# Hybrid attention block on one core: six transpose sources, two maximum tiles, four remainder buffers, remainder products one key tile behind, memory keys and values in reused buffers

## The chip, the core and the metric

The kernel runs on one core of a Trainium2 chip. Its engines are TensorE (PE; its weight loads are listed apart as PEld), VectorE (DVE), ScalarE (ACT), GpSimd (POOL) and SyncE (SP, which here only issues transfers). Each engine works through its own list of instructions in order and waits at an instruction until what it needs is there. The metric is the device time of one launch in microseconds (us).

## What is computed

One decoder layer on x of 2048 tokens by 1024 channels. After a normalisation, one input projection feeds three attention branches and a gate; the branches are concatenated, multiplied by the gate and mapped back.

```python
h = rms_norm(x, norm_g)
cq, ckv, kr, dq, dk, dv, mq, z = split(h @ w_in)
y_mla  = mla_branch(cq, ckv, kr, ...)    # 8 heads, causal, keys of 96, values of 64
y_diff = diff_branch(dq, dk, dv, ...)    # 4 heads, two causal softmax maps each, keys of 32
y_mem  = mem_branch(mq, mem, ...)        # 4 heads over 256 memory tokens
y = concat(y_mla, y_diff, y_mem) * silu(z)
x = x + y @ w_out
```

## The kernel before

**Precision by splitting.** Operands are split into a 16-bit high part and a 16-bit remainder, and a product is made of two or three matmuls.

**Steps.** Attention runs in steps, each for one block of 512 queries (b = 0 to 3): four for the memory branch (m00 to m03), eight for the differential branch (d00 to d13) and sixteen for the latent branch (a00 to a33: four pairs of heads by four blocks). A step first has a preparation (`prep_m`, `prep_d`, `prep_a`): it projects, normalises and rotates, copies queries and keys as 16-bit sources (`ks`, `qs`, and for the other branches `s`, `qa`), turns them with transposing DMAs issued by SP, and estimates row maxima (`est_block`), which are written into the query source before it is transposed a second time. Then come the step's maps, one for each head or softmax map.

**Units.** A map (`class Map`) goes over key tiles of 128. For each one, `head` makes the scores `st` on PE (three matmuls of 512 columns in the latent branch, one in the differential branch), ACT takes the exponential into `p32` (L492), and DVE subtracts its 16-bit view `phi` to leave the remainder `plo` (L493). `tail` then multiplies on PE: eight matmuls of 64 or 65 columns from `phi` (L502, L504) and four from `plo` (L507), all into one accumulator `pv`. Two heads are emitted ahead of each tail (`DEPTH = 2`).

**Rings.** Tiles of one tag share a fixed number of buffers; a tile's first writer waits until the tile that had the buffer is done with. All transpose sources share the tag `s2` with 5 buffers (`stack`). In `prep_a` a source is first touched by POOL, which fills its padding (L855, L861), and then by ACT, which copies the high part (L856 for keys, L862 for queries):

```python
ks = stack([P, 4, 2, P], f"ks{h}_{nm}")
G.memset(ks[:, :, :, 96:128], MS)
A.activation(ks[:, :, 0, 0:96], kn[:, :, h], AF.Copy)
...
qs = stack([P, 2, 4, P], f"qs{h}_{nm}")
G.memset(qs[:, :, :, 96:128], 0.0)
A.activation(qs[:, 0, :, 0:96], q[:, :, h], AF.Copy)
```

The same POOL queue computes the inverse norms `r_a` (L97, L101), for which DVE's scaling of the keys `kn_a` waits (L847). The maximum tile `er` has one buffer: ACT writes the first copy of the estimated scores into it (L390), DVE takes maxima over it (L394, L398, L399). `plo` has three buffers, `p32` three, `st` two, `pv` one. The pool `kvp` has two rings of five: `kT` (transposed keys, `qA` of the memory branch, early weight stages) and `V`.

**Order.** Work outside the maps (preparations, projections, output products) is cut into pieces with planned positions, and the pieces are interleaved with the units by position and priority. From that the framework's scheduler sets the order of each engine's list when the kernel is built, so a change of buffers or of emission order changes the order of all lists.

The memory branch's keys `mk1`, `mk2` and values `mv` lie in buffers of their own for the whole kernel.

Of the kernel before, what the change touches and what calls it, by code (L numbers as in the profile page):

```python
# [11 lines left out]
F32 = mybir.dt.float32  # L12
F16 = mybir.dt.float16
BF16 = mybir.dt.bfloat16
# [5 lines left out]
P = 128  # L20
# [20 lines left out]
def hybrid_block(ctx: ExitStack, tc: tile.TileContext, x, mem, positions, norm_g, w_in, mla_q_norm_g,  # L41
# [3 lines left out]
    V, A, G, T, SP = nc.vector, nc.scalar, nc.gpsimd, nc.tensor, nc.sync  # L45

    cst = ctx.enter_context(tc.tile_pool(name="cst", bufs=1))
# [8 lines left out]
    ps_v = ctx.enter_context(tc.tile_pool(name="ps_v", bufs=1, space=bass.MemoryType.PSUM))  # L56

    def stack(shape, name):
        return wk.tile(shape, F16, tag="s2", name=name, bufs=5)

    def bigt(shape, name):
        return big.tile(shape, F16, tag="big", name=name)
# [134 lines left out]
    g_mk = gain_row(mem_kn_g, 64, "g_mk")  # L197
    g_mq = gain_row(mem_qn_g, 64, "g_mq")
    V.tensor_tensor(g_mk, g_mk, g_mq, ALU.mult)
    mk1 = cst.tile([P, 2, 4, P], F16, name="mk1")  # L200
    mk2 = cst.tile([P, 2, 4, P], F16, name="mk2")
    mv = cst.tile([P, 2, 4, 130], F16, name="mv")

    mem_left = [0]

    def mem_kv():
        units = []
        xts = []
        for t in range(2):
            xts.append(fetch_rows(mem[0, t * P:(t + 1) * P, :], f"m{t}", big, MPACE))  # L210
            yield 1.0
        yield from load_w(w_mem_kv, [(0, 512)], gm, "mkv", units, kvp, pace=MPACE)
        hts = []
        for t in range(2):
            hts.append(normed_t(xts[t], f"m{t}"))
            yield 1.0
        kv = tmp4("mem_kv").rearrange("p (t c) -> p t c", t=2)
        for t in range(2):
            ps = ps_p.tile([P, 512], F32, tag="pp", name="pp")
            project(ps, hts[t], units, 512)  # L220
            A.activation(kv[:, t, :], ps, AF.Copy, scale=1.0 / WS)
            yield 5.0
        sq = tmp4("mem_sq")[:, 0:512].rearrange("p (t c) -> p t c", t=2)
        A.activation(sq, kv[:, 0:2, 0:256], AF.Square, scale=1.0 / 8.0)
        ss = sm.tile([P, 8], F32, tag="yss", name="mem_ss")
        V.reduce_sum(ss[:, 0:8], sq.rearrange("p t (h d) -> p (t h) d", d=64), axis=AX.X)
        r = rstd_of(ss[:, 0:8], [8], "mem_r", "rstd_x")
        kn = tmp4("mem_kn")[:, 0:512].rearrange("p (t h d) -> p t h d", t=2, d=64)
        rr = _bc(r.rearrange("p (t h) -> p t h", h=4), 3, 64)
        V.tensor_tensor(kn, kv[:, 0:2, 0:256].rearrange("p t (h d) -> p t h d", d=64), rr, ALU.mult)  # L230
        kn = kn.rearrange("p t h d -> p (t h) d")
        V.tensor_tensor(kn, kn, _bc(g_mk, 1, 8), ALU.mult)
        s1 = stack([P, 8, 2, 64], "mem_s1")
        s2 = stack([P, 8, 128], "mem_s2")
        A.activation(s1, _bc(kn, 2, 2), AF.Copy)
        V.tensor_tensor(s2[:, :, 0:64], kn, s1[:, :, 0, :], ALU.subtract)
        G.memset(s2[:, :, 64:128], MS)
        SP.dma_start_transpose(mk1.rearrange("p t h k -> p (t h) k"), s1.rearrange("p a b c -> p (a b c)"))
        SP.dma_start_transpose(mk2.rearrange("p t h k -> p (t h) k"), s2.rearrange("p a c -> p (a c)"))
        vv = kv[:, 0:2, 256:512].rearrange("p t (h d) -> p t h d", d=64)  # L240
        A.activation(mv[:, :, :, 0:64], vv, AF.Copy)
        V.tensor_tensor(mv[:, :, :, 65:129], vv, mv[:, :, :, 0:64], ALU.subtract)
        G.memset(mv[:, :, :, 64:65], WS)
        mem_left.clear()
        yield 1.0
# [127 lines left out]
    def est_block(st, i, nmap, mcol, lhs, rhs):  # L373
        b = st.b
        mx = sm.tile([P, nmap, 4, 2], F32, tag="mx", name=f"mx{i}_{st.name}", bufs=2)
        fold = b >= EB
        for m in range(nmap):
            for t in range(4):
                if fold and t % 2 == 0:
                    er = wk.tile([P, 2, 512], BF16, tag="er", name="er", bufs=1)  # L380
                for c in range(b + 1):
                    ps = ps_e.tile([P, 512], F32, tag="pe", name="pe")
                    n = (4 if c < b else t + 1) * P
                    T.matmul(ps[:, 0:n], lhsT=lhs(m, t), rhs=rhs(m, c, n // P), start=True, stop=c < b)  # L384
                    if c == b:
                        T.matmul(ps[:, t * P:n], lhsT=ident, rhs=mask_e, start=False, stop=True)
                    if not fold:
                        V.reduce_max(mx[:, m, t, c:c + 1], ps[:, 0:n], axis=AX.X)
                    elif c == 0:
                        A.activation(er[:, t % 2], ps, AF.Copy)  # L390
                    else:
                        ec = wk.tile([P, 512], BF16, tag="ec", name="ec", bufs=3)
                        A.activation(ec[:, 0:n], ps[:, 0:n], AF.Copy)  # L393
                        V.tensor_tensor(er[:, t % 2, 0:n], er[:, t % 2, 0:n], ec[:, 0:n], ALU.max)  # L394
                    yield 0.5
                if fold and t % 2:
                    for n in (256, 128, 64):
                        V.tensor_tensor(er[:, :, 0:n], er[:, :, 0:n], er[:, :, n:2 * n], ALU.max)  # L398
                    V.reduce_max(mx[:, m, t - 1:t + 1, 0], er[:, :, 0:64], axis=AX.X)  # L399
        if b == 1 and not fold:  # L400
            mr = sm.tile([P, nmap * 4], F32, tag="mr", name=f"mr{i}_{st.name}", bufs=2)
            V.reduce_max(mr, mx.rearrange("p m t c -> p (m t) c"), axis=AX.X)
            mr = mr.rearrange("p (m t) -> p m t", t=4)
        else:
            mr = mx[:, :, :, 0]
        for m in range(nmap):
            V.tensor_scalar_mul(mcol(m), mr[:, m, :], -1.0 / MS)
# [66 lines left out]
    class Map:  # L474
# [9 lines left out]
        def head(self, j):  # L484
            t0 = max(0, j - self.diag0)
            n = (4 - t0) * P
            ps = ps_s.tile([P, 512], F32, tag="st", name="st")
            self.scores(ps, j, t0, n, j >= self.diag0)
            p32 = wk.tile([P, 512], F32, tag="p32", name="p32", bufs=3)
            plo = wk.tile([P, 512], F16, tag="plo", name="plo", bufs=3)  # L490
            phi = p32.bitcast(BF16).rearrange("p (n t) -> p n t", t=2)[:, :, 1]
            A.activation(p32[:, :n], ps[:, :n], AF.Exp, scale=self.scale)  # L492
            V.tensor_tensor(plo[:, :n], p32[:, :n], phi[:, :n], ALU.subtract)  # L493
            return t0, phi, plo

        def tail(self, j, t0, phi, plo):
            if j == 0:
                self.pv = ps_v.tile([P, 4, P], F32, tag="pv", name="pv")
            pvv, vt = self.pv, self.vtile(j)
            for t in range(t0, 4):  # L500
                c = slice((t - t0) * P, (t - t0 + 1) * P)
                T.matmul(pvv[:, t, 0:65], lhsT=phi[:, c], rhs=vt[:, 0:65], start=(j == 0 and t == 0), stop=False,  # L502
                         skip_group_check=True)
                T.matmul(pvv[:, t, 0:64], lhsT=phi[:, c], rhs=vt[:, 65:129], start=False, stop=False, skip_group_check=True)  # L504
            for t in range(t0, 4):
                c = slice((t - t0) * P, (t - t0 + 1) * P)
                last["pv"] = T.matmul(pvv[:, t, 0:65], lhsT=plo[:, c], rhs=vt[:, 0:65], start=False,  # L507
                                      stop=(j == self.njt - 1), skip_group_check=True)
            if j < self.njt - 1:
                return None  # L510
            rl = sm.tile([P, 4], F32, tag="rl", name="rl", bufs=4)
            V.reciprocal(rl, pvv[:, :, 64])
            return self.done(pvv[:, :, 0:64], rl)

    def new_ys(ct, b):
        return wk.tile([P, 2, 4, P], F16, tag="ys", name=f"ys{ct}_{b}", bufs=1)
# [106 lines left out]
    def est_m(st):  # L623
# [6 lines left out]
        for i in range(2):  # L630
            for t in range(4):
                ps = ps_e.tile([P, 512], F32, tag="pe", name="pe")
                for k in range(2):
                    T.matmul(ps[:, 256 * k:256 * k + 256], lhsT=st.qA[:, i, t, k, :], rhs=mk1[:, :, 2 * i + k, :],
                             start=(k == 0), stop=(k == 1), skip_group_check=True)
                V.reduce_max(mx[:, i, t, :], ps.rearrange("p (i k) -> p i k", i=2), axis=AX.X)
                yield 0.5
# [6 lines left out]
    def maps_m(st):  # L644
# [7 lines left out]
        for h in range(4):  # L652

            def scores(ps, j, t0, n, diag, h=h):
                T.matmul(ps, lhsT=mk1[:, j, h, :], rhs=st.qA[:, h // 2, :, h % 2, :], start=True, stop=False)
                T.matmul(ps, lhsT=mk2[:, j, h, :], rhs=st.qB[h // 2][:, :, h % 2, :], start=False, stop=True)

            def done(o, rl, h=h):
                hp, i = h // 2, h % 2
# [578 lines left out]
```

## Time and profile before

| | |
|---|---|
| median of 3 runs | 1416.08 us (1415.18 to 1417.94) |
| profiled execution | 1417.06 us, its span 1415.3 us |
| PE busy | 1309.6 us, 93% of the span |
| DVE busy | 1117.0 us, 79% |
| ACT busy | 898.2 us, 63% |
| POOL busy | 358.9 us, 25% |
| granted TensorE clock, mean | 0.977 |

The span runs from the first to the last instruction of the profiled execution; 1.8 us of its time lie around it. A busy share is an average over stages. A granted clock of 1.00 is 2.4 GHz, and the other level is 1.2 GHz; a mean between them over a stretch is a share of each.

### The profile page before, as it was taken

What the parts mean: (1) busy time and instruction counts of PE and PEld (TensorE: products, weight loads), DVE (VectorE), ACT (ScalarE), POOL (GpSimd) and SP (SyncE); (2) the same over time, 40 slices, a digit from 0 to 9 for tenths busy, and PEclk for the clock granted to TensorE, in tenths of its full rate; (3) what the DMA queues carried; (4) which work ended last, traced back from release to release, by engine and by line L of the source; (5) the groups of instructions that cost most, each with busy time, mean ns of one, the idle gap of its engine ahead of it and who ended that gap; (6) DMA issues with size and microseconds to landing.
All of it is one profiled execution on the core that took longest, in us unless ns stands there. A gap on an engine that the chain in (4) does not pass through costs nothing.

```text
span 1415.3 us, 35199 instructions
## 1 busy us (share of the span) xinstructions
PE 1309.6 (93%) x13552; PEld 833.7 (59%) x13552; DVE 1117.0 (79%) x2649; ACT 898.2 (63%) x2153; POOL 358.9 (25%) x541
## 2 busy tenths in 40 slices
PE   4889899999999999998998999999998988999998
PEld 1344455667677666667775655666655655565554
DVE  3558787889888867888898888887889987985745
ACT  4646444687787646786885766766776777674521
POOL 2222133304063133104212143252333332300000
PEclk9999999999999999999999999999999998999999
DMA  8999754224213313437345156346434443255452
GB/s 203 252 213 194 163 102 98 53 61 87 55 31 69 69 32 59 76 106 194 113 89 137 47 151 173 69 98 146 117 91 94 115 81 72 54 128 168 130 190 76
DMA packets 302697, 157.67 MB, mean 111 GB/s; under 512 B 248385, under 2 KB 281281, under 8 KB 302529
## 3 DMA queue, kind: packets, MB, share of 16 engines
q1 hardware_dynamic: 302496, 155.42, 46.9%
q8 instruction: 106, 1.74, 0.5%
q14 instruction: 63, 0.51, 0.1%
q0 software_dynamic: 32, 0.00, 0.0%
HBM read 61.79 MB, written 34.34 MB: 68 GB/s over the span
## 4 chain that ended last, share of the span: by engine, by line
PE 51%; DMA 12%; DVE 12%; POOL 11%; ACT 8%; issue 5%; SPq 2%; ACTq 0%; DVEq 0%; POOLq 0%
PE pp L176 6%; PE pp L177 5%; PE pp L178 5%; PE pe L384 5%; DMA kT_a<-ks_a 3%; DVE plo L493 3%; PE pv L507 3%; PE pv L504 3%; PE pp L932 3%; PE pv L502 3%; PE pp L934 3%; PE pp L933 3%; PE st L548 2%; POOL r_a L101 2%; PE st L892 2%
## 5 line engine op out<-in xcount | busy, mean ns | idle before, releaser
L492 ACT ACTIVATE p<-st 128x512 f32<-128x512 f32 (+3 forms) x672 | 356.4, 547 | 183.1 <-PE st L894 64.5
L493 DVE TENSOR_TENSOR plo<-p 128x512 f16<-128x512 f32 (+3 forms) x672 | 406.7, 616 | 63.0 <-ACT p L492 54.0
L393 ACT ACTIVATE ec<-pe 128x512 bf16<-128x512 f32 (+3 forms) x384 | 198.3, 534 | 35.8 <-PE pe L384 14.8
L502 PEld LDWEIGHTS <-p 128*128 128x128 bf16 x2304 | 186.7, 100 | 47.3 <-issue 7.4
L504 PEld LDWEIGHTS <-p 128*128 128x128 bf16 x2304 | 177.2, 99 | 31.3 <-issue 2.1
L507 PEld LDWEIGHTS <-plo 128*128 128x128 f16 x2304 | 135.3, 99 | 56.5 <-DVE plo L493 22.4
L394 DVE TENSOR_TENSOR er<-er,ec 128x512 bf16<-128x512 bf16 (+3 forms) x384 | 143.7, 380 | 30.3 <-ACT ec L393 20.3
L390 ACT ACTIVATE er<-pe 128x512 bf16<-128x512 f32 x192 | 110.4, 606 | 39.7 <-DVE mx_d L399 13.9
L176 PEld LDWEIGHTS <-ht_x 128*128 128x128 f16 x896 | 88.1, 98 | 73.2 <-DMA ht_x<-xh_x 21.1
L892 PE MATMUL st<-qB_a,kT_a 97*128 97x512 f16 (+1 forms) x320 | 113.0, 353 | 18.4 <-ACT p L492 17.2
L502 PE MATMUL pv<-V_d,p 128*128 128x65 f16 x1088 | 119.9, 195 | 2.7 <-DVE y_d L559 2.4
L177 PEld LDWEIGHTS <-ht_x 128*128 128x128 f16 x896 | 88.2, 98 | 57.3 <-issue 11.8
L548 PE MATMUL st<-qB_d,kT_d 97*128 97x512 f16 (+1 forms) x320 | 112.5, 355 | 9.9 <-ACT p L492 8.8
L504 PE MATMUL pv<-V_d,p 128*128 128x64 f16 x1088 | 120.0, 197 | 0.0
L178 PEld LDWEIGHTS <-ht_x 128*128 128x128 f16 x896 | 88.1, 98 | 53.8 <-issue 4.1
L502 PE MATMUL pv<-V_a,p 128*128 128x65 f16 x1088 | 116.5, 194 | 1.2 <-ACT p L492 0.9
L504 PE MATMUL pv<-V_a,p 128*128 128x64 f16 x1088 | 116.2, 196 | 0.0
L893 PE MATMUL st<-qB_a,kT_a 96*128 96x512 f16 (+1 forms) x320 | 113.1, 354 | 0.0
L894 PE MATMUL st<-qB_a,kT_a 96*128 96x512 f16 (+1 forms) x320 | 112.4, 351 | 0.0
L384 PE MATMUL pe<-kT_d,qB_d 96*128 96x512 f16 (+2 forms) x320 | 106.6, 351 | 5.9 <-ACT ec L393 2.9
L384 PE MATMUL pe<-kT_a,qB_a 96*128 96x512 f16 (+2 forms) x320 | 102.0, 358 | 6.9 <-DMA qB_a<-qs_a 3.1
L507 PE MATMUL pv<-V_a,plo 128*128 128x65 f16 x1088 | 89.5, 195 | 9.6 <-DVE plo L493 9.2
(285 smaller groups left out, 3363.7 us busy)
## 6 DMA issues: line engine op xcount, KB each, us to landing
xt_x<-in_x_dram SPq DMA_DIRECT2D x16, 512.0 KB, 4.7
xr<-in_x_dram SPq DMA_DIRECT2D x16, 512.0 KB, 3.6
part<-xr SPq DMA_DIRECT2D x16, 512.0 KB, 2.9
ysc<-yt SPq DMA_DIRECT2D x31, 256.0 KB, 2.2
yl<-ysc SPq DMA_DIRECT2D x15, 512.0 KB, 4.3
zsc<-zc SPq DMA_DIRECT2D x48, 128.0 KB, 2.1
xa<-part SPq DMA_DIRECT2D x12, 512.0 KB, 3.6
out_dram<-xa SPq DMA_DIRECT2D x12, 512.0 KB, 2.9
```

The source lines that it names most:

```text
L176: T.matmul(ps[:, :n], lhsT=ht[:, 0, k], rhs=wt[:, 0, :n], start=(k == 0), stop=False)
L177: T.matmul(ps[:, :n], lhsT=ht[:, 0, k], rhs=wt[:, 1, :n], start=False, stop=False)
L178: T.matmul(ps[:, :n], lhsT=ht[:, 1, k], rhs=wt[:, 0, :n], start=False, stop=(k == NK - 1))
L384: T.matmul(ps[:, 0:n], lhsT=lhs(m, t), rhs=rhs(m, c, n // P), start=True, stop=c < b)
L393: A.activation(ec[:, 0:n], ps[:, 0:n], AF.Copy)
L394: V.tensor_tensor(er[:, t % 2, 0:n], er[:, t % 2, 0:n], ec[:, 0:n], ALU.max)
L492: A.activation(p32[:, :n], ps[:, :n], AF.Exp, scale=self.scale)
L493: V.tensor_tensor(plo[:, :n], p32[:, :n], phi[:, :n], ALU.subtract)
L502: T.matmul(pvv[:, t, 0:65], lhsT=phi[:, c], rhs=vt[:, 0:65], start=(j == 0 and t == 0), stop=False, skip_group_check=True)
L504: T.matmul(pvv[:, t, 0:64], lhsT=phi[:, c], rhs=vt[:, 65:129], start=False, stop=False, skip_group_check=True)
L507: last["pv"] = T.matmul(pvv[:, t, 0:65], lhsT=plo[:, c], rhs=vt[:, 0:65], start=False, stop=(j == self.njt - 1), skip_group_check=True)
L892: T.matmul(ps[:, :n], lhsT=kt[0:97, h, j % 4, 0, :], rhs=q[0:97, 0, t0:4, :], start=True, stop=False)
```

## The change

Five edits. The transpose sources get six buffers, `er` two and `plo` four. In `tail`, the four `plo` products of a key tile are no longer issued behind that tile's `phi` products but behind those of the next tile; the last tile of a map issues both (new method `low`). The memory keys become one tile `mk12` in the ring `kT` and the values a tile in the ring `V`. No instruction is added or removed on any engine: the numbers of matmuls, vector, scalar and GpSimd operations and transfers are the same.

```diff
     def stack(shape, name):
-        return wk.tile(shape, F16, tag="s2", name=name, bufs=5)
+        return wk.tile(shape, F16, tag="s2", name=name, bufs=6)
...
-    mk1 = cst.tile([P, 2, 4, P], F16, name="mk1")
-    mk2 = cst.tile([P, 2, 4, P], F16, name="mk2")
-    mv = cst.tile([P, 2, 4, 130], F16, name="mv")
+    mk = []
+    mv = kvp.tile([P, 2, 4, 130], F16, tag="V", name="mv", bufs=5)
...
+        mk12 = kvp.tile([P, 2, 2, 4, P], F16, tag="kT", name="mk12")
+        mk.extend([mk12[:, 0], mk12[:, 1]])
...
-                    er = wk.tile([P, 2, 512], BF16, tag="er", name="er", bufs=1)
+                    er = wk.tile([P, 2, 512], BF16, tag="er", name="er", bufs=2)
...
-            plo = wk.tile([P, 512], F16, tag="plo", name="plo", bufs=3)
+            plo = wk.tile([P, 512], F16, tag="plo", name="plo", bufs=4)
...
+            if self.late is not None:
+                self.low(*self.late)
+            self.late = (j, t0, plo)
+            if j < self.njt - 1:
+                return None
+            self.low(*self.late)
+            rl = sm.tile([P, 4], F32, tag="rl", name="rl", bufs=4)
+            V.reciprocal(rl, pvv[:, :, 64])
+            return self.done(pvv[:, :, 0:64], rl)
+
+        late = None
+
+        def low(self, j, t0, plo):
+
+            pvv, vt = self.pv, self.vtile(j)
             for t in range(t0, 4):
                 c = slice((t - t0) * P, (t - t0 + 1) * P)
                 last["pv"] = T.matmul(pvv[:, t, 0:65], lhsT=plo[:, c], rhs=vt[:, 0:65], start=False,
                                       stop=(j == self.njt - 1), skip_group_check=True)
```

**First place, PE in step a13.** The matmuls of PE's list around two key tiles of one map; tiles are named by their numbers, and the exponential and the remainder of one key tile have neighbouring numbers (`p32_18319` and `plo_18320`). Weight loads and the further `phi` and `plo` products of a tile are left out. Before:

```order
L502 MATMUL pv_18283<-V_a10_14947,p32_18319 128x65
L504 MATMUL pv_18283<-V_a10_14947,p32_18319 128x64
...
L507 MATMUL pv_18283<-V_a10_14947,plo_18320 128x65
...
L892 MATMUL st_18389<-qB1_a13_17066,kT_a11_15928 128x512
L893 MATMUL st_18389<-qB1_a13_17066,kT_a11_15928 128x512
L894 MATMUL st_18389<-qB1_a13_17066,kT_a11_15928 128x512
```

Now, the same key tile (its remainder is `plo_18315` here, its exponential was used a row group earlier):

```order
L505 MATMUL pv_18282<-V_a11_15799,p32_18342 128x64
L523 MATMUL pv_18282<-V_a10_14942,plo_18315 128x65
...
L903 MATMUL st_18450<-qB1_a13_17062,kT_a11_15923 128x512
L904 MATMUL st_18450<-qB1_a13_17062,kT_a11_15923 128x512
L905 MATMUL st_18450<-qB1_a13_17062,kT_a11_15923 128x512
...
L503 MATMUL pv_18282<-V_a11_15799,p32_18368 128x65
...
L523 MATMUL pv_18282<-V_a11_15799,plo_18343 128x65
```

Behind the `phi` products of one tile there now stand the `plo` products of the tile before it, so a remainder is wanted one whole unit (three score matmuls, eight `phi` and four `plo` products) later than it was.

**Second place, ACT in step a20.** The copies into the transpose sources of a20 in ACT's list, with some of the exponentials between them. Before:

```order
L856 ACTIVATE ks0_a20_18008<-kn_a20_17567 128x4x96
...
L492 ACTIVATE p32_16564<-st_16560 128x512
L862 ACTIVATE qs0_a20_18033<-qkv_a20_17566 128x4x96
L492 ACTIVATE p32_16594<-st_16590 128x512
...
L856 ACTIVATE ks1_a20_18059<-kn_a20_17567 128x4x96
...
L862 ACTIVATE qs1_a20_18118<-qkv_a20_17566 128x4x96
```

Now:

```order
L873 ACTIVATE qs0_a20_18028<-qkv_a20_17561 128x4x96
L493 ACTIVATE p32_16532<-st_16528 128x512
...
L867 ACTIVATE ks0_a20_18003<-kn_a20_17562 128x4x96
...
L867 ACTIVATE ks1_a20_18054<-kn_a20_17562 128x4x96
...
L873 ACTIVATE qs1_a20_18113<-qkv_a20_17561 128x4x96
```

The first query copy of a20 has moved ahead of the first key copy; before, it stood a few instructions behind it.

**Third place, POOL in the same step.** The paddings of the sources and the inverse norm `r_a20` in POOL's list. Before:

```order
L855 MEMSET ks0_a20_18008 128x8x32
...
L101 TENSOR_TENSOR r_a20_17852<-r_a20_17852,mhalf_97 128x16
L842 TENSOR_TENSOR kn_a20_17567<-krot0_6706,r_a20_17852 128x8x32
L861 MEMSET qs0_a20_18033 128x8x32
L855 MEMSET ks1_a20_18059 128x8x32
```

Now:

```order
L866 MEMSET ks0_a20_18003 128x8x32
L872 MEMSET qs0_a20_18028 128x8x32
...
L101 TENSOR_TENSOR r_a20_17849<-r_a20_17849,mhalf_97 128x16
L853 TENSOR_TENSOR kn_a20_17562<-krot0_6701,r_a20_17849 128x8x32
L866 MEMSET ks1_a20_18054 128x8x32
L872 MEMSET qs1_a20_18113 128x8x32
```

The padding of the first query source has moved ahead of the inverse norm: one more source is claimed early.

## Rows read from the trace of the kernel before

**Rows 1.** The page, part 1: busy time, share, instructions of each engine.

```profile
PE 1309.6 (93%) x13552; PEld 833.7 (59%) x13552; DVE 1117.0 (79%) x2649; ACT 898.2 (63%) x2153; POOL 358.9 (25%) x541
```

**Rows 2.** Stretches of the span: busy us by engine, granted clock, DMA share, GB/s.

```profile
core 0: us, PE busy (x) PEld busy (x) DVE busy (x) ACT busy (x) POOL busy (x), PEclk, DMA share, GB/s
...
750.00:800.00 50.00, 42.83 (x589) 28.81 (x586) 43.32 (x108) 32.95 (x79) 3.17 (x9) 0.90 0.38 80
1150.00:1200.00 50.00, 44.02 (x495) 28.11 (x495) 40.40 (x97) 36.79 (x89) 15.39 (x22) 0.88 0.33 59
1350.00:1400.00 50.00, 50.00 (x459) 27.57 (x458) 23.20 (x41) 11.89 (x22) 0.00 (x0) 1.00 0.28 100
```

**Rows 3.** Waits over the whole span: us in total, times, longest.

```profile
ACT qs_a L862 <- DMA kT_a<-ks_a: 30.2, 14, 4.4
...
PE st L892 <- ACT p L492: 17.2, 16, 2.9
...
ACT er L390 <- DVE mx_d L399: 13.9, 12, 3.2
PE pv L507 <- DVE plo L493: 12.6, 16, 2.3
ACT er L390 <- DVE mx_a L399: 12.6, 13, 3.3
...
PE st L548 <- ACT p L492: 8.8, 12, 3.5
...
PE pe L384 <- ACT er L390: 0.7, 2, 0.4
```

**Rows 4.** Timeline of PE, 906 to 911 us: start, us, instruction, idle before.

```profile
906.65 0.38 PE L892 MATMUL st<-qB_a,kT_a 97*128 97x512 f16 x1
906.87 0.38 PE L893 MATMUL st<-qB_a,kT_a 96*128 96x512 f16 x1
...
910.16 0.30 PE L507 MATMUL pv<-V_a,plo 128*128 128x65 f16 x4 [2.34 <-DVE plo L493]
910.29 0.19 PE L502 MATMUL pv<-V_a,p 128*128 128x65 f16 x1
...
910.60 0.19 PE L504 MATMUL pv<-V_a,p 128*128 128x64 f16 x1
910.63 0.19 PE L502 MATMUL pv<-V_a,p 128*128 128x65 f16 x1
```

**Rows 5.** Timeline of DVE, 907 to 910 us.

```profile
907.52 0.69 DVE L847 TENSOR_TENSOR kn_a<-kn_a,r_a 128x512 f32<-128x512 f32 x1 [3.15 <-POOL r_a L101]
908.13 1.37 DVE L850 TENSOR_TENSOR qkv_a<-qkv_a,r_a 128x768 f32<-128x768 f32 x1
909.42 0.68 DVE L493 TENSOR_TENSOR plo<-p 128x512 f16<-128x512 f32 x1
```

**Rows 6.** Timeline of POOL, 895 to 908 us.

```profile
898.25 0.31 POOL L861 MEMSET qs_a<- 128x256 f16 x1 [17.57 <-DMA qB_a<-qs_a]
...
904.56 2.93 POOL L101 TENSOR_TENSOR r_a<-r_a,mhalf 128x16 f32<-128x16 f32 x1
```

**Rows 7.** Timeline of ACT, 764 to 770 us.

```profile
768.39 0.52 ACT L862 ACTIVATE qs_a<-qkv_a 128x384 f16<-128x384 f32 x1 [4.41 <-DMA kT_a<-ks_a]
...
769.18 0.60 ACT L492 ACTIVATE p<-st 128x512 f32<-128x512 f32 x1
```

**Rows 8.** Timeline of PE, three of its waits for ACT.

```profile
769.84 0.59 PE L548 MATMUL st<-qB_d,kT_d 97*128 97x512 f16 x1 [3.51 <-ACT p L492]
...
1002.91 0.38 PE L892 MATMUL st<-qB_a,kT_a 97*128 97x512 f16 x1 [1.93 <-ACT p L492]
...
1221.39 0.20 PE L502 MATMUL pv<-V_a,p 128*128 128x65 f16 x1 [0.89 <-ACT p L492]
```

**Rows 9.** The page, part 5: groups by line; busy us, mean ns, idle before.

```profile
L492 ACT ACTIVATE p<-st 128x512 f32<-128x512 f32 (+3 forms) x672 | 356.4, 547 | 183.1 <-PE st L894 64.5
...
L393 ACT ACTIVATE ec<-pe 128x512 bf16<-128x512 f32 (+3 forms) x384 | 198.3, 534 | 35.8 <-PE pe L384 14.8
```

**Rows 10.** Timeline of PE: the eighth score matmul of the memory branch, m00's last.

```profile
128.80 0.38 PE L655 MATMUL st<-qA_m,mk 128*128 128x512 f16 x1
```

**Rows 11.** The tile kT_d: its transposes; durations in ns, first and last start.

```profile
L460 SPq DMA_TRANSPOSE kT_d<-s_d x16: 1232/1239/2030, 199.1 to 654.0; - x16
```

More of the change, by code (lines that the diff above doesn't have):

```diff
@@ L237, in mem_kv @@
         G.memset(s2[:, :, 64:128], MS)
-        SP.dma_start_transpose(mk1.rearrange("p t h k -> p (t h) k"), s1.rearrange("p a b c -> p (a b c)"))
-        SP.dma_start_transpose(mk2.rearrange("p t h k -> p (t h) k"), s2.rearrange("p a c -> p (a c)"))
+        mk12 = kvp.tile([P, 2, 2, 4, P], F16, tag="kT", name="mk12")
+        mk.extend([mk12[:, 0], mk12[:, 1]])
+        SP.dma_start_transpose(mk[0].rearrange("p t h k -> p (t h) k"), s1.rearrange("p a b c -> p (a b c)"))
+        SP.dma_start_transpose(mk[1].rearrange("p t h k -> p (t h) k"), s2.rearrange("p a c -> p (a c)"))
         vv = kv[:, 0:2, 256:512].rearrange("p t (h d) -> p t h d", d=64)
@@ L508, in tail @@
                                       stop=(j == self.njt - 1), skip_group_check=True)
[L509 to L513, printed above, removed]
     def new_ys(ct, b):
@@ L633, in est_m @@
                 for k in range(2):
-                    T.matmul(ps[:, 256 * k:256 * k + 256], lhsT=st.qA[:, i, t, k, :], rhs=mk1[:, :, 2 * i + k, :],
+                    T.matmul(ps[:, 256 * k:256 * k + 256], lhsT=st.qA[:, i, t, k, :], rhs=mk[0][:, :, 2 * i + k, :],
                              start=(k == 0), stop=(k == 1), skip_group_check=True)
@@ L654, in scores @@
             def scores(ps, j, t0, n, diag, h=h):
-                T.matmul(ps, lhsT=mk1[:, j, h, :], rhs=st.qA[:, h // 2, :, h % 2, :], start=True, stop=False)
-                T.matmul(ps, lhsT=mk2[:, j, h, :], rhs=st.qB[h // 2][:, :, h % 2, :], start=False, stop=True)
+                T.matmul(ps, lhsT=mk[0][:, j, h, :], rhs=st.qA[:, h // 2, :, h % 2, :], start=True, stop=False)
+                T.matmul(ps, lhsT=mk[1][:, j, h, :], rhs=st.qB[h // 2][:, :, h % 2, :], start=False, stop=True)
             def done(o, rl, h=h):
```

## The prediction

> **What bounds the kernel now.** I read the busy shares first: PE is busy 93% of the span, no other engine over 79% [rows 1]. Then the stretches of 50 us: late in the span PE is busy for all 50 us at a granted clock of 1.00, while 750 to 800 and 1150 to 1200 us have 42.8 and 44.0 us of PE work at 0.90 and 0.88 [rows 2]. So PE's list is the bound, and what can be won is the time that it stands still or runs at the lower level ahead of that full tail; time saved there brings the end forward, since nothing behind it waits for anything else. The view of waits says for whom PE stands still: 26.0 us for an exponential ahead of new scores (17.2 in the latent branch, 8.8 in the differential one) and 12.6 us in 16 places for the remainder `plo` [rows 3]. The timelines say why each is late, and the reasons differ.
>
> **The remainder.** At 910.16 PE stands 2.34 us ahead of four `plo` products [rows 4]. DVE had waited 3.15 us for the inverse norm, then did a scaling of 0.69 and one of 1.37 us, and only then the subtraction [rows 5]. The norm in turn was late on POOL, whose list had stood 17.57 us at the padding of a query source, waiting for a buffer of the transpose ring [rows 6]. So DVE is late by other work that stands ahead of the subtraction; the exponentials are not.
>
> **The exponential.** At 768.39 ACT starts a query copy after 4.41 us of waiting for the transpose of the key source; the exponential queued behind it starts at 769.18 [rows 7], and PE, 3.51 us late, at 769.84 [rows 8]. ACT has 14 such waits, 30.2 us [rows 3]. Going through PE's waits one by one I find nine of 0.7 us or more that end right behind one, 16.9 us in all, from 769.84 to 1221.39; five of them, 9.6 us, lie before 1003 us [rows 8] (the rows are the first, the fifth and the last). The buffers explain the 14: if sources claim buffers in POOL's order and give them back in the order of SP's last transposes, then in the list of before exactly 14 query sources of the latent branch take over the buffer of the key source just ahead of them in the same step, so the copy waits for a transpose that has only just been issued.
>
> **The sum, part by part**, against the profiled execution's 1417.1 us (span 1415.3 and 1.8 around it).
>
> *Remainder products one tile later, four buffers.* Of PE's work, a unit of the latent branch is three score matmuls at 0.22 us from start to start, eight `phi` products at 0.03 and four `plo` products in 0.13 [rows 4], about 1.03 us; that is how much later a remainder is now wanted. A unit of the differential branch has one score matmul, 0.60 us. The 16 waits are 0.79 us long in the mean [rows 3], so most would be covered; the longest, 2.34 us, would leave 1.3, and two others in the latent branch pass 1.03 us by 0.4 together. That keeps about 2 of 12.6 us: minus 11 us, with bounds of 0 (all of it reappears at another wait) and minus 15. The outer bound comes from how the idle time is counted: a score matmul is listed with 0.38 us but the next starts 0.22 behind it, a 65-column one with 0.19 and 0.03 [rows 4], so each of 16 waits may cost 0.16 us more than its idle time. The Trainium skill (Perfetto Trace Analysis, section Tensor Engine Instruction) says of this that the end of a matmul in a profile is estimated, not observed; by idle time alone the bound would be 12.6, by starts it is 15, and the trace sides with the starts. The fourth buffer only pays for the delay: each remainder is held one unit longer.
>
> *Six transpose sources.* The sixth buffer doesn't end the waiting, because POOL's list claims it at once, padding one source further ahead (the third place shown with the change). Counted in the same way, the tight pairs fall from 14 to 9. Those that go lie in a01 to a20, those that stay in a21 to a32. I take PE's waits before 1003 us as gone, minus 9 us; bounds 0 (they only move) and minus 17 (all nine).
>
> *The clock.* The two stretches at 0.90 and 0.88 lack 0.10 and 0.12 of 50 us [rows 2], 11 us of full speed, and both hold the longest ACT waits. A part of the shortfall lies in the idle time itself. With the first stretch's waits gone and the second's kept I take minus 4; bounds 0 and minus 10.
>
> *Two maximum tiles.* ACT waits 26.5 us (13.9 and 12.6) for DVE's maxima before it may write `er` again [rows 3]. But PE stood only 0.7 us for such a copy [rows 3]; ACT has little else to do when it waits there. Minus 1, with bounds of 0 and of minus 3, the longest single wait.
>
> *Memory keys and values in the rings.* The key ring is now full with `mk12` and four `qA`, so d00's keys need the buffer of m00's `qA`. Its last score matmul is at 128.80 [rows 10], the first transposes of `kT_d` at 199.1 [rows 11]: 70 us of cover, so nothing. PE's list up to there is the same. If that cover were gone, d00's key transposes would be late by as much as m00's last scores come after 199.1, once. The value ring holds `mv` and the four tiles of d00 to d03, which is five. Nothing for both.
>
> *New waits.* With the `plo` products displaced, the `phi` products stand closer behind their scores: in the differential branch 41 units instead of 11 have less than 1.2 us of PE work between the end of their scores and the first `phi` product (counted in the lists with the spacing above). An undisturbed exponential needs 0.55 us [rows 9] and the score's tail 0.16; if a copy of 0.53 us [rows 9] stands ahead on ACT, the sum passes 1.2. I take a quarter of the 30 units at 0.53: plus 4; bounds 0 and plus 16.
>
> Sum: minus 11, 9, 4 and 1, plus 4: minus 21, so 1396 for an execution like the profiled one. The median of before lies 1.0 us under that execution, so **1395 us**.
>
> **Rivals.** *The wait moves on.* PE no longer stands at `plo` but at the next scores or `phi` products, because ACT, held up by ring waits, is late at the same places; the shifted lists give a new mixture. For it: PE's larger wait is for ACT, 26.0 against 12.6 us, and the ring stays full. Against it: at 910 the exponentials were done. Gains are then 2 for the remainder and 4 for the ring: 1411 us less 1.0, 1410.
>
> *All the ring's waits go.* Sixteen-bit sources with one more buffer are enough, all nine PE waits and both slow stretches vanish: minus 11, 17, 10 and 1, plus 4, is minus 35: 1381. Against it: the nine tight pairs left in the lists. The Trainium skill (Trainium Kernel Development and Optimization, section Best Practices) says that consistent bubbles can mean that on-chip memory ran out; the trace agrees that ACT's 30.2 us are waits for a buffer, and by that rule alone this case would be the forecast.
>
> *No change.* The five edits' gains are given back by other orders, within 0.2% of before, which is about what a measurement of this kernel can tell.
>
> *Slower.* The `phi` products become the wait: each of the 30 closer units in the differential branch stands a whole copy, 16 us, and the latent branch, where units with less than 2.5 us of cover rise from 59 to 96, the same for 37 more, 20 us. Against the 25 us of gains that is plus 11, 1427. It decides once about 47 of these 67 units wait 0.53 us each. Against it: of 672 units of before, PE stood at `phi` for an exponential once for 0.89 us [rows 8], though 11 units were that close.
>
> **Chances.** Forecast 50%, its own range 1387 to 1404. The wait moves on 22%, nearly all of it between 1404 and 1413. All ring waits gone 12%, 1374 to 1387. No change 7%. Slower 9%. Faster by over 0.2%: 50, 12 and most of 22, together 0.82; the same, 0.09; slower, 0.09. The range that leaves out 2 in 10 goes from 1380 to 1413.
>
> **What would show it.** In the profile of after, PE's wait at the `plo` products should fall from 12.6 us to 1 to 3. ACT's wait at query copies for key transposes should be near 20 us in 8 to 10 places, late in the span, and PE's 26.0 us for exponentials ahead of scores near 16. ACT's wait for the maxima should be gone. The stretch after 750 us should show a clock nearer 1. PE's wait at the `phi` products should be under 5 us. I'm wrong if the plo wait is gone and the time isn't: then the waits for ACT will have grown by as much. I'm also wrong if POOL's longer reach ahead delays the inverse norms, which would show as a DVE wait at the key scaling above before's.

## The result and the profile after

The changed kernel takes 1398.21 us, median of four executions (1394.3 to 1403.92), against 1416.28 us for the kernel before: a ratio of 0.988 with a 95% interval from 0.9844 to 0.9915. That is 18.1 us less, where 21 were forecast. The profiled execution of after is the slowest of its four, 1403.92 us, so the two profiles differ by 13.1 us only. Two executions that took more than twice as long as the others, one of the kernel before and one of a run below (e10), are left out of all ratios and means here.

Part 1 of the page of after: busy time, share and instructions of each engine, which answers to [rows 1].

```profile
PE 1303.8 (93%) x13552; PEld 830.8 (59%) x13552; DVE 1111.0 (79%) x2649; ACT 898.9 (64%) x2153; POOL 352.1 (25%) x541
```

The work is the same, as the counts say. The span of 1402.0 us less PE's busy time leaves 98.2 us in which PE stands still, against 105.7 before. So of the 13.3 us by which the two profiled spans differ, 7.5 are time in which PE stood and 5.8 are PE's own busy time.

The waits of after over the whole span (us in total, times, longest), which answer to [rows 3]; the lines moved by up to 16 (L492 is now L493, L507 is L523, L548 is L559, L862 is L873, L892 is L903).

```profile
PE st L903 <- ACT p L493: 10.2, 14, 1.6
PE pv L523 <- DVE plo L494: 8.7, 8, 2.3
PE pe L385 <- DMA qB_a<-qs_a: 8.6, 9, 2.8
PE st L559 <- ACT p L493: 4.7, 9, 1.5
...
PE pv L503 <- DVE y_d L566: 3.9, 4, 3.1
...
PE pp L825 <- DVE V_a L357: 3.0, 3, 2.5
...
ACT qs_a L873 <- DMA kT_a<-ks_a: 8.2, 8, 2.4
...
ACT er L391 <- DVE mx_d L400: 1.4, 2, 1.1
...
DVE kn_a L858 <- POOL r_a L101: 14.7, 11, 2.8
```

ACT's waits for key transposes fell from 30.2 to 8.2 us and those for the maxima from 26.5 to 1.8 (1.4 in this row, 0.4 in one that isn't shown). The eight waits for key transposes that are left end between 958.80 and 1147.17 us. PE's waits for exponentials ahead of scores fell from 26.0 to 14.9, for remainders from 12.6 to 8.7. Against that stand waits that had been small: 8.6 us for the transposed queries `qB_a` (3.1 before), 5.4 for outputs of the branches (3.0), 4.4 ahead of the products of L825 (0.4).

The stretches of after (busy us by engine, granted clock, DMA share, GB/s), which answer to [rows 2]:

```profile
core 0: us, PE busy (x) PEld busy (x) DVE busy (x) ACT busy (x) POOL busy (x), PEclk, DMA share, GB/s
400.00:450.00 50.00, 46.25 (x716) 39.93 (x714) 47.70 (x127) 35.44 (x89) 16.26 (x26) 0.93 0.41 69
650.00:700.00 50.00, 45.06 (x520) 34.39 (x518) 38.57 (x91) 39.51 (x97) 5.93 (x12) 0.93 0.50 138
750.00:800.00 50.00, 42.60 (x615) 28.90 (x614) 41.22 (x96) 34.61 (x81) 2.12 (x9) 0.97 0.37 80
1150.00:1200.00 50.00, 45.35 (x555) 28.80 (x553) 48.03 (x117) 39.24 (x92) 21.17 (x29) 1.00 0.34 67
...
```

The two stretches that I had pointed at, 0.90 and 0.88 before, now show 0.97 and 1.00. But 400 to 450 and 650 to 700 us, at 1.00 and 0.97 before, show 0.93. The low clock moved. Each is one execution, though: over the executions of before alone the mean clock runs from 0.974 to 0.989.

A remainder can still be late by the old cause. Timelines of after round 1035 us (start, us, instruction, idle before), first PE:

```profile
1035.17 0.29 PE L523 MATMUL pv<-V_a,plo 128*128 128x65 f16 x4 [2.31 <-DVE plo L494]
```

then DVE:

```profile
1032.09 0.81 DVE L858 TENSOR_TENSOR kn_a<-kn_a,r_a 128x512 f32<-128x512 f32 x1 [1.10 <-POOL r_a L101]
1032.82 1.07 DVE L861 TENSOR_TENSOR qkv_a<-qkv_a,r_a 128x768 f32<-128x768 f32 x1
1033.81 0.70 DVE L399 TENSOR_TENSOR er<-er 128x256 bf16<-128x256 bf16 x1
1034.43 1.28 DVE L494 TENSOR_TENSOR plo<-p 128x512 f16<-128x512 f32 x2
```

and ACT:

```profile
1035.20 0.60 ACT L493 ACTIVATE p<-st 128x512 f32<-128x512 f32 x1 [2.62 <-DVE plo L494]
```

As at 910 us before [rows 5], DVE stands for the inverse norm, then scales, and only then subtracts. ACT too stands 2.62 us, since its next exponential needs the `p32` buffer that DVE hasn't read yet.

### The profile page after: what moved, and what is told of

Read it like the earlier page. It is cut to its first block, busy times and chain, and to the rows that moved or that the text cites. A ratio compares the mean times of both kernels' runs of the same rounds, so it can differ in the third digit from the quotient of the medians.

```text
span 1402.0 us, 35085 instructions
## 1 busy us (share of the span) xinstructions
PE 1303.8 (93%) x13552; PEld 830.8 (59%) x13552; DVE 1111.0 (79%) x2649; ACT 898.9 (64%) x2153; POOL 352.1 (25%) x541
## 4 chain that ended last, share of the span: by engine, by line
PE 59%; DVE 13%; DMA 10%; POOL 6%; ACT 5%; issue 4%; SPq 2%; ACTq 0%; DVEq 0%; POOLq 0%
PE pp L176 6%; PE pp L177 6%; PE pp L178 6%; PE pe L385 6%; PE pv L505 4%; PE pv L503 3%; DVE plo L494 3%; PE pv L523 3%; PE pp L943 3%; PE pp L945 3%; PE pp L944 3%; DMA qB_a<-qs_a 3%; PE st L559 3%; PE st L903 3%; PE st L904 2%
## 5 line engine op out<-in xcount | busy, mean ns | idle before, releaser
L493 ACT ACTIVATE p<-st 128x512 f32<-128x512 f32 (+3 forms) x672 | 356.3, 548 | 210.3 <-PE st L905 81.4
L394 ACT ACTIVATE ec<-pe 128x512 bf16<-128x512 f32 (+3 forms) x384 | 196.1, 538 | 29.5 <-PE pe L387 11.7
L503 PEld LDWEIGHTS <-p 128*128 128x128 bf16 x2304 | 185.6, 100 | 48.6 <-DVE y_d L566 7.4
L505 PEld LDWEIGHTS <-p 128*128 128x128 bf16 x2304 | 172.3, 98 | 39.9 <-issue 2.9
L523 PEld LDWEIGHTS <-plo 128*128 128x128 f16 x2304 | 120.8, 98 | 24.6 <-DVE plo L494 12.8
L391 ACT ACTIVATE er<-pe 128x512 bf16<-128x512 f32 x192 | 118.0, 617 | 24.0 <-PE pe L385 20.7
L903 PE MATMUL st<-qB_a,kT_a 97*128 97x512 f16 (+1 forms) x320 | 113.4, 354 | 11.2 <-ACT p L493 10.2
L503 PE MATMUL pv<-V_d,p 128*128 128x65 f16 x1088 | 115.8, 194 | 5.3 <-DVE y_d L566 3.9
L559 PE MATMUL st<-qB_d,kT_d 97*128 97x512 f16 (+1 forms) x320 | 112.0, 353 | 5.4 <-ACT p L493 4.7
L505 PE MATMUL pv<-V_d,p 128*128 128x64 f16 x1088 | 115.8, 196 | 0.0
L503 PE MATMUL pv<-V_a,p 128*128 128x65 f16 x1088 | 111.0, 193 | 0.0
L505 PE MATMUL pv<-V_a,p 128*128 128x64 f16 x1088 | 110.8, 195 | 0.0
L385 PE MATMUL pe<-kT_d,qB_d 96*128 96x512 f16 (+2 forms) x320 | 102.9, 350 | 5.8 <-DMA qB_d<-s_d 2.8
L385 PE MATMUL pe<-kT_a,qB_a 96*128 96x512 f16 (+2 forms) x320 | 93.6, 349 | 12.4 <-DMA qB_a<-qs_a 8.6
L176 PE MATMUL pp<-w_d,ht_x 128*128 128x512 f16 x256 | 97.0, 379 | 0.3 <-ACT ql L185 0.3
```

Of the source, the lines that this page charges most:

```text
L176: T.matmul(ps[:, :n], lhsT=ht[:, 0, k], rhs=wt[:, 0, :n], start=(k == 0), stop=False)
L559: T.matmul(ps[:, :n], lhsT=st.kTs[j // 4][0:97, h, j % 4, m % 2, :], rhs=st.qB[h][0:97, t0:4, m % 2, :], start=True, stop=not diag)
L903: T.matmul(ps[:, :n], lhsT=kt[0:97, h, j % 4, 0, :], rhs=q[0:97, 0, t0:4, :], start=True, stop=False)
```

## The experiments

Each kernel ran beside executions of before on the same chip, against which its ratio stands.

### First four: single edits on before

All of them have the memory keys and values in the rings, which e1 has alone.

```diff
 e1: - mk1, mk2, mv in cst          + mk12 in ring kT, mv in ring V
 e2: e1 and  - tag="s2", bufs=5     + tag="s2", bufs=6
 e3: e1 and  - tag="er", bufs=1     + tag="er", bufs=2
 e4: e1 and  - plo products in the same tail, bufs=3
             + plo products one tile later (low), bufs=4
```

> Of the five edits only the one that puts the memory keys and values into the rings. Theory of the prediction (three named waits were won): no change, within 3 us of before, the wait for the remainder near 12.6 us and ACT's wait of query copies for key transposes near 30 us, since its order of instructions hardly differs. Rival (any change of buffers reorders all lists, and the gain is luck of the order): it moves by 5 us or more either way.

Measured: 1415.67 against 1417.0 us, 0.9991 [0.9967, 1.0015]. The rings cost nothing.

> The memory edit and six transpose sources, no other. Theory: minus 9 us against before (minus 5 to minus 14), ACT's wait of query copies for key transposes from 30 to 8 to 20 us, PE's wait for exponentials ahead of scores from 26 to 15 to 20, the wait for the remainder still near 12 us. Rival that all of the gain is the late remainder: no change. Rival of the order: anything, and PE's waits move between lines without that pattern.

Measured: 1426.48 us, 1.0062 [1.004, 1.0084], slower. The waits of e2:

```profile
PE pv L520 <- DVE plo L494: 14.8, 14, 4.4
PE st L900 <- ACT p L493: 13.7, 15, 2.3
...
ACT qs_a L870 <- DMA kT_a<-ks_a: 11.1, 9, 2.9
```

The sixth buffer does what was forecast to ACT, 30.2 to 11.1 us in nine places, and the time still rises, against both the theory and the rival of no change. PE's waits that end within 2 us behind the start of a query copy that had waited for a key transpose are 17.5 us in before and 1.9 in e2. But PE stands 113.0 us in e2's profile, against 105.7: longer for remainders (14.8, before 12.6), for transposed queries (7.2, before 3.1) and ahead of the products of L822 (4.3, before 0.4).

> The memory edit and two maximum tiles, no other. Theory: minus 1 us, at most 3; ACT's wait of 26.5 us for the maxima goes below 4 us, yet PE's waits stay as before. Rival that a waiting ACT holds back exponentials wherever it waits: minus 8 or more.

Measured: 1412.57 us, 0.9967 [0.9945, 0.9989], a little faster.

> The memory edit, the remainder products one key tile later and four remainder buffers; five transpose sources and one maximum tile. Theory: minus 7 us against before (minus 3 to minus 11), the wait for the remainder from 12.6 to under 9 us. Rival that the wait moves on: the wait for the remainder falls by as much, and PE's waits for exponentials (26.0 us) rise by it, time within 3 us of before.

Measured: 1421.93 us, 1.0039 [1.0017, 1.0061], slower. The waits of e4:

```profile
PE pv L523 <- DVE plo L494: 17.4, 13, 4.1
PE st L903 <- ACT p L493: 17.4, 20, 2.5
...
ACT qs_a L873 <- DMA kT_a<-ks_a: 23.0, 15, 3.6
```

The late remainder alone leaves fewer waits (13 for 16), but longer ones: 17.4 us, more than before's 12.6; the theory and the rival both missed. Eight of the 13, 11.3 us, come as at 910 us before: POOL stood at the padding of a source, and DVE then for the norm. One of the eight, in the timelines of POOL, DVE and PE:

```profile
896.10 0.31 POOL L872 MEMSET qs_a<- 128x256 f16 x1 [13.49 <-DMA qB_a<-qs_a]
...
902.70 2.93 POOL L101 TENSOR_TENSOR r_a<-r_a,mhalf 128x16 f32<-128x16 f32 x1
...
905.66 0.69 DVE L858 TENSOR_TENSOR kn_a<-kn_a,r_a 128x512 f32<-128x512 f32 x1 [3.16 <-POOL r_a L101]
...
908.64 0.29 PE L523 MATMUL pv<-V_a,plo 128*128 128x65 f16 x4 [1.74 <-DVE plo L494]
```

The longest of the 13 has another cause, a norm of the differential branch. POOL had waited 46.50 us for DVE's sums there, and not for the ring:

```profile
386.83 10.42 POOL L101 TENSOR_TENSOR r_d<-r_d,mhalf 128x32 f32<-128x32 f32 x1
...
397.28 0.80 DVE L444 TENSOR_TENSOR qkv_d<-qkv_d,r_d 128x512 f32<-128x512 f32 x1 [5.34 <-POOL r_d L101]
...
398.94 0.40 PE L523 MATMUL pv<-V_d,plo 128*128 128x65 f16 x4 [4.11 <-DVE plo L494]
```

In after the same norm takes 5.93 us, at 390.81, and PE doesn't wait there. Why it took 10.42 us here is not shown.

With e1's part taken out of the other three, the four edits multiply to 0.9% slower (0.9991 by 1.0071, 0.9976 and 1.0048); all at once are 1.2% faster. So the edits don't add, as far as one order each can tell.

### Second four: one edit less than after, and an order that means nothing

```diff
 e5: after with   - plo products one tile later, bufs=4   + in the same tail, bufs=3
 e6: after with   - tag="s2", bufs=6    + tag="s2", bufs=5
 e7: after with   - tag="er", bufs=2    + tag="er", bufs=1
 e8: before with  - LEAD = 11.0         + LEAD = 11.5
```

`LEAD` is a constant of the planner: how far ahead of a step its preparation is to be done. It changes no instruction and no buffer, only the order of the lists.

> The changed kernel with the remainder products back behind their own tile (and three remainder buffers): memory edit, six sources, two maximum tiles. Alone, these gave +0.62% (six sources) and -0.33% (maximum tiles). If single effects add up: about +0.3%, 1421 us. If the sixth source is only worth something once ACT no longer stands at the maximum tile: -0.5% or better, 1410 or less. If order alone decides: anything between -0.6 and +0.6%.

Measured: 1418.61 against 1416.9 us, 1.0016 [0.9994, 1.0039]. That fits the adding up (+0.3%), and not a sixth source that a second maximum tile makes worth something.

> The changed kernel with five transpose sources: memory edit, late remainder, two maximum tiles. Added up from the single runs: +0.06%, 1418 us. Interplay theory (six sources carry the gain once the others are in): +0 to +0.3%. If order alone decides: anything between -0.6 and +0.6%.

Measured: 1413.75 us, 0.9982 [0.9961, 1.0003]. The waits of e6:

```profile
PE st L903 <- ACT p L493: 19.5, 15, 3.6
...
PE pv L523 <- DVE plo L494: 5.6, 7, 1.8
...
ACT qs_a L873 <- DMA kT_a<-ks_a: 21.7, 9, 5.3
```

The remainder is down to 5.6 us of PE's waits; with five sources ACT is late again, and PE behind it: its waits right behind such query copies, counted as in e2, are 11.5 us here and 2.9 in after.

> The changed kernel with one maximum tile: memory edit, late remainder, six sources. Added up from the single runs: +1.0%, 1431 us. Interplay theory: between before and that, as ACT's 25 us at the maximum tile stay. Prediction's theory (named waits, maxima worth 1 us): -1.1%, 1400.

Measured: 1412.88 us, 0.9971 [0.9958, 0.9985], neither the added +1.0% nor the -1.1% of the prediction's theory. The waits of e7:

```profile
ACT er L391 <- DVE mx_d L400: 16.5, 14, 2.3
...
ACT er L391 <- DVE mx_a L400: 9.9, 10, 4.7
```

> The kernel before with the planner's constant LEAD at 11.5 in place of 11.0, which only shifts planned positions and so the order of all lists: no buffer, no product, no wait is changed on purpose. If waits with a cause decide the time, it stays within 0.2% of before (1413 to 1420). If the order that the scheduler happens to make is worth as much as the edits, it moves by 0.4% or more either way.

Measured: 1425.56 us, 1.0074 [1.0048, 1.0101]. This order, which means nothing, costs more than any single edit won or lost. None of e1 to e7 can then be read by its ratio alone.

### Last four: both kernels at other orders, and after with three remainder buffers

```diff
 e9:  after with   - LEAD = 11.0   + LEAD = 11.5
 e10: after with   - LEAD = 11.0   + LEAD = 10.5
 e11: before with  - LEAD = 11.0   + LEAD = 10.5
 e12: after with   - tag="plo", bufs=4   + tag="plo", bufs=3
```

> The changed kernel with LEAD at 11.5, to be set against the kernel before with LEAD at 11.5 (+0.74%). If the five edits together win something that doesn't hang on one order: 0.5 to 1.8% under that kernel, so -1.0 to +0.2% against before. If the -1.2% was a lucky order: no better than before with the same constant, +0.4% or more.

Measured: 1413.72 against 1415.47 us, 0.9978 [0.9952, 1.0004].

> The changed kernel with LEAD at 10.5, to be set against the next run. Edits win apart from the order: 0.5% or more under it. Lucky order: the two within 0.4% of each other or the other way round.

Measured: 1408.99 us, 0.9953 [0.9927, 0.998].

> The kernel before with LEAD at 10.5. Either theory: between -0.7 and +0.8% of before, since LEAD at 11.5 moved it by +0.74%.

Measured: 1416.54 us, 1.0003 [0.9978, 1.0028].

So with the same `LEAD` on both sides the edits give 0.995 (10.5), 0.988 (11.0) and 0.9905 (11.5, each side by its own comparison with before): a win at all three orders, about 0.9% in the mean. With the half-widths of the two ratios added by squares, the pair at 10.5 has an interval from 0.991 to 0.999, that at 11.5 from 0.987 to 0.994.

> The changed kernel with three remainder buffers in place of four. If the fourth buffer is what lets the remainder be late: the subtraction on DVE, and behind it other DVE work, now waits for PE's products of three tiles before, and the time rises by 0.5% or more against the changed kernel (-0.7% or worse against before). If it isn't needed: within 0.5% of the changed kernel, which is what another order does anyway.

Measured: 1394.19 us, 0.9857 [0.9825, 0.9889], not to be told apart from after. The waits of e12:

```profile
DVE plo L494 <- PE pv L523: 12.6, 15, 3.8
...
PE pv L523 <- DVE plo L494: 5.0, 7, 2.1
```

With three buffers DVE stands 12.6 us for a free one, and PE doesn't notice. The fourth buffer is not needed.

### All kernels in one account

The scatter has a place. For each execution I multiply the span by its mean granted clock, which gives the span at full clock, and call the rest what the clock lacks; the table has the means over all executions of a kernel (4 to 10; of before the 76 that ran beside e1 to e12, in three batches that lie at 1385.2 to 1386.3 us at full clock). PE's and ACT's waits are from the one profiled execution, which for e9 was the longest of its ten. All but before, e8 and e11 have the memory keys and values in the rings.

| kernel | late | s2 | er | LEAD | span | clock lacks | at full clock | PE for plo (times) | ACT for key transposes |
|---|---|---|---|---|---|---|---|---|---|
| before | no | 5 | 1 | 11 | 1414.2 | 28.6 | 1385.6 | 12.6 (16) | 30.2 |
| e1 | no | 5 | 1 | 11 | 1413.4 | 28.0 | 1385.4 | 12.7 (18) | 29.5 |
| e2 | no | 6 | 1 | 11 | 1424.9 | 39.0 | 1385.9 | 14.8 (14) | 11.1 |
| e3 | no | 5 | 2 | 11 | 1410.5 | 24.4 | 1386.1 | 14.1 (13) | 11.7 |
| e4 | yes | 5 | 1 | 11 | 1420.4 | 35.1 | 1385.3 | 17.4 (13) | 23.0 |
| e5 | no | 6 | 2 | 11 | 1417.3 | 31.5 | 1385.9 | 10.8 (14) | 8.5 |
| e8 | no | 5 | 1 | 11.5 | 1424.7 | 34.9 | 1389.8 | 15.2 (16) | 21.6 |
| e11 | no | 5 | 1 | 10.5 | 1415.3 | 28.9 | 1386.5 | 16.4 (26) | 12.5 |
| e6 | yes | 5 | 2 | 11 | 1412.0 | 31.5 | 1380.5 | 5.6 (7) | 21.7 |
| e7 | yes | 6 | 1 | 11 | 1411.3 | 35.3 | 1376.1 | 9.6 (8) | 6.6 |
| e9 | yes | 6 | 2 | 11.5 | 1410.8 | 31.0 | 1379.8 | 19.9 (12) | 5.4 |
| e10 | yes | 6 | 2 | 10.5 | 1405.8 | 26.7 | 1379.1 | 8.5 (9) | 8.8 |
| after | yes | 6 | 2 | 11 | 1396.8 | 30.4 | 1366.5 | 8.7 (8) | 8.2 |
| e12 | yes | 6 | 2 | 11 | 1392.6 | 26.5 | 1366.1 | 5.0 (7) | 6.0 |

The standard errors of the column at full clock are 0.4 to 1.8 us. Three things stand in it. The single edits, and both buffer edits together (e5), leave the time at full clock where it was, 1385.3 to 1386.1: the 10.7 us lost in e2, the 6.2 lost in e4 and the 3.7 won in e3 are nearly all the clock's by this product. The late remainder together with at least one buffer edit lowers it in all six kernels, to 1366.1 to 1380.5, below all eight others. And with all edits it lies 13 us apart between orders (after 1366.5, e9 1379.8, e10 1379.1), more than e6, e7 and after say about single buffers.

One caution: within a kernel, an execution with a clock higher by 0.001 is shorter by 0.75 us in the mean, and not by the 1.4 that this product takes. With 0.75 the two sets still stand apart (at a clock of 0.980, 1412.5 us and more against 1410.3 and less), but only by 2 us, and e2 and e4 keep about 5 and 3 us of their loss.

## Why the prediction was right, and where not

**The sum** was nearly right, minus 18 for minus 21, within the forecast's own range. Part of that is luck: at three orders, equal on both sides, the edits win 19.1, 10.0 and 7.4 us at full clock, 12 in the mean; the other 6 us go with this one order. The parts were not met either: PE's waits for remainders fell by 3.9 us where 11 were forecast, its waits right behind late query copies by 14.6 (17.5 to 2.9) where 9 were, and three other waits of PE rose by 11.9 where 4 were.

**Adding parts** is the step that failed. I priced the late remainder at 11 us and the six sources at 9, each alone, and at the one order that ran either alone gives nothing (e4 and e2, at full clock minus 0.3 and plus 0.3); together (e7) they give 9.5. In e2 the waits that I had priced are gone, and PE stands longer elsewhere. In e4 the working at 910 us applies in a way that I hadn't used: the norm is late because POOL stands at the full ring, so the remainder hangs on the ring too, and one unit of cover is too little for eight such waits. That is the rival in which the wait moves on, at work for each edit alone. In e6 the reverse stands: the remainder is mostly covered, and the full ring reaches PE by ACT (11.5 us of PE's waits). That each edit uncovers the other's wait fits these rows; that it is the whole reason was not shown, since the lists are made anew with the buffers, and no run could hold the order while a buffer changed. The late remainder without a buffer edit ran at one order only, and with all edits orders differ by 13 us, so e4 alone doesn't settle what it is worth; the six kernels against the eight weigh more.

**The remainder.** Forecast: PE's wait falls from 12.6 to 1 to 3 us. It is 8.7. I took the 16 waits as fixed and set one unit against each, and left out what this leaves of two waits of the differential branch (1.62 and 0.92 us against a unit of 0.60), 1.3 us more. Over the seven kernels of either kind, the times fall from 16.7 to 9.1 in the mean (without late 16, 18, 14, 13, 14, 16, 26; with 13, 7, 8, 12, 9, 8, 7), the total only from 13.8 to 10.7 us. So there are fewer waits, and those left are longer in the mean (1.2 for 0.8 us); the long ones whose timelines are shown, at 399 us in e4 and at 1035 us in after, have a norm behind them. And the fourth buffer doesn't "pay for the delay": e12.

**Six sources.** Forecast: ACT's wait near 20 us in 8 to 10 places, PE's for exponentials near 16. It is 8.2 in 8 places, and 14.9. The count that came from the order of the lists held, and so did the place, late in the span; the waits left over are shorter than those of before. The Trainium skill (Trainium Kernel Development and Optimization, section Best Practices) says that consistent bubbles can mean that on-chip memory ran out; the traces agree for ACT, 30.2 to 11.1 us by one buffer (e2), and not for the time, which rose by 0.62%. The rival that rested on it, 1381 us, is refuted for this order, although what it asked of PE's waits nearly came true (17.5 to 2.9 us): ending them did not bring that time.

**The clock.** Forecast minus 4. What the clock lacks went from 28.6 to 30.4 us in the means, with a standard error of about 2 us for after's four executions, and from 32.6 to 30.8 in the two profiled ones: no gain of 4 is shown. The two stretches did rise, others fell. I had read a cause out of two stretches of one execution, and not rightly: of ACT's waits for key transposes the second longest, 4.21 us at 1001.86, lies in neither, but in a stretch at 0.97. Across kernels the lack runs from 24.4 to 39.0 us with the order.

**Two maximum tiles.** The wait is gone as forecast (26.5 to 1.8; with one tile in e7 26.4). Alone it wins nothing at full clock (e3); as the last edit it wins 9.6 (e7 to after), which lies within the 13 us between orders, and e7 has the wait of 4.1 us near 400 us that e4 has and after hasn't. Its price stays open.

**Memory keys and values.** Nothing, as forecast (e1).

**New waits.** Forecast plus 4, at the `phi` products. PE has no wait of after at L503 or L505 for an exponential, so the rival "slower" had no ground; the place was wrong. PE's waits at L503, forecast under 5 us, are 5.4, all for outputs of the branches. The size was too small: transposed queries, outputs and the products of L825 took 5.5, 2.4 and 4.0 us more, 11.9 together, within the bound of 16.

**Not borne out** was also the fear that POOL's longer reach ahead delays the norms: DVE's wait at the key scaling fell from 18.5 to 14.7 us.

## What to carry to other kernels

Where a scheduler makes all lists anew, a change of a buffer is also a change of order, and here an order without meaning was worth 0.74% on the kernel before and 1.0% on the changed one (0.988 to 0.9978): compare both kernels at several equal orders before an edit gets the credit. Take the span times the granted clock beside the time, for it roughly tells work that was saved from a clock that happened to be better. An edit that looks worthless alone may be half of a pair: two late suppliers of one engine can hide each other, so try them together before either is dropped.

## What was not expected of the chip

The same 13552 matmuls ran at mean granted clocks from 0.9726 (e2, five executions) to 0.9827 (e3, ten), by nothing but order and buffers. In e2 eight of the 27 stretches of 50 us between 50 and 1400 us have a granted clock under 0.97, before three and e12 two. Four of e2's stretches:

```profile
1100.00:1150.00 50.00, 40.37 (x465) 27.77 (x463) 41.18 (x91) 34.13 (x85) 23.06 (x34) 0.90 0.44 97
1150.00:1200.00 50.00, 45.65 (x580) 29.90 (x579) 43.03 (x108) 37.89 (x92) 11.95 (x18) 1.00 0.33 71
1200.00:1250.00 50.00, 45.80 (x554) 28.36 (x551) 45.12 (x110) 35.59 (x76) 9.02 (x16) 0.93 0.28 56
1250.00:1300.00 50.00, 44.05 (x435) 25.23 (x433) 32.78 (x83) 25.55 (x55) 0.31 (x1) 0.93 0.69 157
```

PE is busy 45.65 us at a clock of 1.00 in the second and 45.80 us at 0.93 in the third, so the sum of idle time in a stretch doesn't tell the clock there. Three in e12:

```profile
1050.00:1100.00 50.00, 40.02 (x529) 28.14 (x530) 44.55 (x93) 35.53 (x84) 16.64 (x29) 0.99 0.51 113
1100.00:1150.00 50.00, 47.68 (x556) 31.46 (x555) 44.24 (x122) 43.23 (x105) 13.83 (x17) 0.94 0.45 96
1150.00:1200.00 50.00, 41.31 (x492) 26.22 (x491) 42.93 (x101) 31.00 (x70) 17.77 (x24) 0.93 0.28 55
```

Here PE first stands for 10 us of a stretch at 0.99, and the clock is lower in the stretch behind it, where PE is busy again for 47.68 us. In e2's rows it is the other way: PE stands 9.6 us from 1100 to 1150 us, at 0.90, and the next stretch is at 1.00. Stretches of 10 us of e12 show more:

```profile
1060.00:1070.00 10.00, 5.24 (x64) 3.16 (x64) 8.23 (x17) 7.27 (x13) 2.26 (x6) 1.00 0.71 211
1070.00:1080.00 10.00, 8.41 (x111) 5.73 (x110) 9.87 (x18) 5.35 (x15) 9.53 (x10) 1.00 0.53 93
1080.00:1090.00 10.00, 10.00 (x135) 7.24 (x134) 9.40 (x28) 8.78 (x23) 0.45 (x2) 1.00 0.15 29
1090.00:1100.00 10.00, 6.90 (x108) 4.89 (x107) 7.05 (x13) 5.51 (x13) 3.90 (x9) 0.95 0.54 67
1100.00:1110.00 10.00, 10.00 (x96) 7.38 (x95) 8.02 (x19) 7.30 (x23) 5.64 (x7) 0.71 0.24 55
```

The clock begins to fall in the fourth, where PE is busy for 6.90 us, and is at 0.71 in the fifth, where PE is busy throughout; in the first PE is busy for only 5.24 us, and the clock stays at 1.00 there and in the two behind it. So a stretch's clock has to be read with what PE did ahead of it, and even that doesn't tell these two pauses apart: why the clock fell at the one and not at the other, no run here shows.
